# Handing over the spread of a norm's root one dense output behind the root, in a hybrid decoder block on Trainium2

## The chip, the core and the metric

The kernel runs on one core of one Trainium2 chip. A core has five engines that work side by side, each through its own instructions in order: TensorE (matmul; "PE" in the profile, "PEld" for its weight loads), VectorE ("DVE"), ScalarE ("ACT"), GpSimd ("POOL") and SyncE ("SP", which issues most DMAs). The metric is the device time of one execution in microseconds, less is better. Before the change it is 1903.87 us, the median of three runs (1902.76 to 1906.84).

## What is computed

One layer of a decoder on a sequence of 2048 tokens with 1024 features, all in float32. The reference, cut to the layer itself:

```python
hn = rmsnorm(h, norm1_g)
proj = jnp.einsum('bsd,de->bse', hn, w_in)          # u_pool | q | k | v, 512 each
y_pool = pool_mixer(u_pool, pool_w, pool_scale)     # causal means over 2, 4, 8, 16 tokens
o = stick_breaking_attention(to_heads(q), to_heads(k), to_heads(v))   # 8 heads of 64
mixed = jnp.concatenate([rmsnorm(y_pool, pool_out_g), rmsnorm(y_attn, attn_out_g)], axis=-1)
h = h + jnp.einsum('bse,ed->bsd', mixed, w_out)
hn2 = rmsnorm(h, norm2_g)
act = jnp.square(jax.nn.relu(jnp.einsum('bsd,df->bsf', hn2, w_up)))
h = h + jnp.einsum('bsf,fd->bsd', act, w_down)
return rmsnorm(h, final_g)
```

with `rmsnorm(x, g) = x * rsqrt(mean(x * x) + 1e-6) * g` over the features of a token.

## The kernel before

**Tiling.** The tokens are cut into four blocks j = 0 to 3 of 512. A tile holds 128 features by 512 tokens, so a block is eight such chunks. A float32 operand is split into a high part and a rest (`split`, lines 145 and 146: a ScalarE copy and a VectorE difference), and a product takes three matmuls of the parts (lines 177 to 179). A *dense output* is one chunk of an output: 8 x 3 matmuls into one PSUM buffer of the pool `psd`, which has two, and an evacuation of it. One step of the program makes one dense output.

**Phases.** `front(0)` projects blocks 0 and 1 (30 steps), `front(1)` blocks 2 and 3 (32 steps). The attention over near tokens (`near`), in units of two query blocks, is woven in between the dense outputs. `tail` multiplies by w_out, block after block (4 x 8 steps, evacuation on line 813). Then come the up and down products of the feed-forward part, some 1200 us, which the change does not touch.

**A norm.** The squares of the chunks are added up (`add_square`, lines 184 to 188). `mean_squares` sums over the features with eight small matmuls (`pm`, line 204). `inv_root` takes the inverse root: line 212 on VectorE fetches m from PSUM, and lines 213 to 223 are 13 small steps on GpSimd. Lines 240 and 241 split the root into `yr`. The *spread* (`spread`, line 230) is eight matmuls that copy each token's root to all 128 partitions (`pr`, in PSUM), and line 250 copies that on ScalarE to `r`. All this is `inv_rms`. The pieces that use r follow: `normed` (line 262: product with gain and root on VectorE, then a split and, for pool and attention norms, a write to `mx` on SP's queue) or the products of `norm2` (line 828). Thirteen norms have their root on GpSimd through `inv_rms`: norm1 of blocks 1, 2, 3, the pool norms and the attention norms of all four blocks, and norm2 of blocks 0 and 1. The first norm is on VectorE; norm2 of blocks 2 and 3 goes through `root_last`, and the final norms have code of their own.

**What sets the order.** Work that is not urgent goes as closures into the list `later`. After each step, `catch_up` takes some of them from its front: `state["pieces"]` (1, 2 or 3 by phase), but at least 2 while the list holds more than 8. At the ends of phases a note flushes the list whole. What a closure traces is put behind two earlier instructions on their engines (`issue_after`): the latest weight split and the evacuation of the output before the last. After `catch_up`, `advance` traces attention units, to be issued behind the last matmul of the step. The program is not run in the order of tracing: a planner that simulates the core's engines gives each engine its order beforehand. It prefers what was traced earlier, except that what is traced under `tc.high_priority()` comes as if from the program's start. All of `inv_rms` is traced so. `state["tick"]` counts up by 2 with a step. `gates` are bounds on the other side: no matmul of a dense output beyond that tick may be issued ahead of the named one (`pm` 10 ticks behind its root, `pr` 14). The PSUM buffers of `pr` come from `pst` (tag `pt`, two buffers, shared with the attention's transposes `pta`), or from `psz` with `early`.

Further names in the prediction: `pls` is the split pooled input of `pool_group` (matmuls on lines 396 to 398), `vf` and `ptv` a v chunk and its transposes (`keep_v`, lines 437 and 440), `sums_first` (lines 850 to 857) makes sums of normed chunks and writes them to `su`, which the up product reads as `sr`.

Of the kernel before, what the change touches and what calls it, by code (L numbers as in the profile page):

```python
# [17 lines left out]
D = 1024  # L18
# [27 lines left out]
def hymba_block(ctx: ExitStack, tc: tile.TileContext, xT, gains, w_in, pool_w, w_out, w_up, w_down, out):  # L46
    nc = tc.nc
# [103 lines left out]
    later = []  # L151
    marks, gates = {}, []
# [37 lines left out]
    def sum_tile():  # L190
        return tmp.tile([P, T], F32, tag="ss", name="ss", bufs=2)
# [7 lines left out]
    def mean_squares(parts, n, where=None, tag="px"):  # L199

        pm = (where or psx).tile([P, T], F32, tag=tag, name="pm")
        for c in range(TB):
            for i, ss in enumerate(parts):
                marks["pm"] = nc.tensor.matmul(pm[:, c:c + 1], ss[:, c * P:(c + 1) * P], inv[n],
                                               start=(i == 0), stop=(i == len(parts) - 1))
        return pm[:, 0:TB]

    def inv_root(pm, eng):

        v, w = vp.tile([P, 3 * TB], F32, tag="v", name="v"), pm.shape[-1]  # L210
        m, y, t = v[:, 0:w], v[:, TB:TB + w], v[:, 2 * TB:2 * TB + w]
        nc.vector.tensor_scalar(m, pm, 1.0, EPS, op0=ALU.mult, op1=ALU.add)
        eng.tensor_scalar(y.bitcast(I32), m.bitcast(I32), -0.5, float(0x5F3759DF), op0=ALU.mult, op1=ALU.add)
        for _ in range(3):
            if eng is nc.vector:
                eng.scalar_tensor_tensor(t, y, -0.5, y, op0=ALU.mult, op1=ALU.mult)
                eng.tensor_tensor(t, t, m, ALU.mult)
                eng.scalar_tensor_tensor(y, t, 1.5, y, op0=ALU.add, op1=ALU.mult)
            else:
                eng.tensor_tensor(t, y, y, ALU.mult)  # L220
                eng.tensor_tensor(t, t, m, ALU.mult)
                eng.tensor_scalar(t, t, -0.5, 1.5, op0=ALU.mult, op1=ALU.add)
                eng.tensor_tensor(y, y, t, ALU.mult)
        return y
# [9 lines left out]
    def inv_rms(ss, n, r=None, eng=None, early=False):  # L234

        eng = eng or nc.gpsimd
        with tc.high_priority():
            y = inv_root(mean_squares([ss], n, psz if early else None, "pz" if early else "px"), eng)
            yr = tmp.tile([P, 2, TB], F32R, tag="yr", name="yr")
            eng.tensor_copy(yr[:, 0], y)  # L240
            eng.tensor_tensor(yr[:, 1], y, yr[:, 0].bitcast(F32), ALU.subtract)
            where, tag = (psx, "px") if eng is nc.vector else (psz, "pz") if early else (pst, "pt")
            pr = where.tile([P, T], F32, tag=tag, name="pr")
            marks["pr"] = spread(pr, yr)
            if eng is not nc.vector:
                g = state["tick"]
                gates.extend([(g + 10, marks["pm"]), (g + 14, marks["pr"])])
            if r is None:
                r = tmp.tile([P, T], F32, tag="r", name="r", bufs=2)
            nc.scalar.activation(r, pr, AF.Copy)  # L250
            return r

    def rms(chunks):
        return inv_rms(sum_squares(chunks), len(chunks) * P)
# [41 lines left out]
    todo, begun, finished, state = [], {}, set(), {"gran": 0, "tick": 0, "due": 0.0}  # L296


    st = [{} for _ in range(NT)]
# [31 lines left out]
    def root_tile():  # L331
        return pa.tile([P, T], F32, tag="r1", name="r1")
# [15 lines left out]
    def norm1_rms(j):  # L348
        def square(k):
            if k == 0:  # L350
                st[j]["ss"] = sum_tile()
            add_square(st[j]["ss"], st[j]["x"][:, k], k == 0)
        later.extend(lambda k=k: square(k) for k in range(KD))
        later.append(lambda: st[j].update(r=inv_rms(st[j]["ss"], D, root_tile() if j == 2 else None, early=j == 1)))

    def norm1(j):
        st[j]["h"] = normed(KD, lambda k: st[j]["x"][:, k], g1, lambda: make_h(j), lambda: st[j]["r"])
# [48 lines left out]
    def norm_parts(j, part, g, at, make=None):  # L406

        def square(k):
            if k == 0:
                st[j]["sm"] = sum_tile()  # L410
            add_square(st[j]["sm"], part(k), k == 0)
        later.extend(lambda k=k: square(k) for k in range(4))
        where = lambda: olp.tile([P, T], F32, tag="ra", name="ra", bufs=1) if make else None
        later.append(lambda: st[j].update(rm=inv_rms(st[j]["sm"], D // 2, where())))
        if make:
            return lambda: normed(4, part, g, make, lambda: st[j]["rm"])
        normed(4, part, g, make_st, lambda: st[j]["rm"], mx[j][at:at + 4])
# [400 lines left out]
    def root_last(i, ss, where=None, tag="px"):  # L818
        y = inv_root(mean_squares([ss], D, where, tag), nc.gpsimd)
        nc.gpsimd.tensor_copy(yrlast[:, i, 0], y)  # L820
        nc.gpsimd.tensor_tensor(yrlast[:, i, 1], y, yrlast[:, i, 0].bitcast(F32), ALU.subtract)

    def norm2(j):
        acc = [st[j]["acc"][:, k] for k in range(KD)]
        later.append(lambda: root_last(0, st[j]["sh"]) if j == 2 else st[j].update(rh=inv_rms(st[j]["sh"], D)))

        def put(k):
            nc.vector.scalar_tensor_tensor(acc[k], acc[k], g2[:, k:k + 1], st[j]["rh"], op0=ALU.mult, op1=ALU.mult)
        if j in PAIRS[0]:
            later.extend(lambda k=k: put(k) for k in range(KD))  # L830
# [654 lines left out]
        if not todo:  # L1485
            state["due"] = 0.0

    def catch_up(n):
        for _ in range(n):
            with ExitStack() as behind:  # L1490
                for ins in (last_split[0], done[0]):
                    if ins:
                        behind.enter_context(tc.issue_after(ins.ins))
                later.pop(0)()

    def run():
        for n, emit, again in prog:
            if n:
                if again:
                    w = grans[state["gran"] - n:state["gran"]]  # L1500
                else:
                    w = weights(state["gran"], n)
                    state["gran"] += n
                state["tick"] += n
                with ExitStack() as behind:
                    for gate in [g for g in gates if g[0] < state["tick"]]:
                        behind.enter_context(tc.issue_after(gate[1].ins))
                        gates.remove(gate)
                    emit(w)
                catch_up(min(len(later), max(state["pieces"], 2 if len(later) > 8 else 1)))  # L1510
                advance(n / 2 * state["ratio"])
            else:
                emit()
        prog.clear()
# [61 lines left out]
    front(1)  # L1576
    tail(True)
    run()
    ffn()


    count = P * H * (TB * NT - 2)
    got = nc.values_load(zeros[0:1, 0:1], min_val=0, max_val=count)
# [59 lines left out]
```

## Time and profile before

| | us |
|---|---|
| time, median of three runs | 1903.87 |
| time of the profiled execution | 1905.2 |
| its span, first to last instruction | 1903.5 |
| granted TensorE clock over the span | 0.994 |
| the GpSimd roots' spreads, first and last start | 68.83 and 617.22 |

The page gives busy time and share by engine. A row of the timeline gives start, length, engine, line and operation, output and inputs, how many instructions it merges, and in brackets the idle time of the engine before it with what ended that. A row of the list of waits gives who waited for whom, the sum in us, the number of times and the longest. A row of the windows gives, for a stretch of the span, its length, each engine's busy time with its instructions (PE, PEld, DVE, ACT, POOL), the granted clock of TensorE (1.00 is full), the mean share of busy DMA engines and GB/s. Matmuls overlap, so a matmul's own length is longer than the distance to the next.

### The profile page before, as it was taken

The page shows a single profiled execution, that of the slowest core. Times are in us where ns is not written, and L with a number is a line of the kernel's source. Part 1 is how long each engine was busy: PE and PEld are TensorE (multiplying, and loading weights), DVE is VectorE, ACT ScalarE, POOL GpSimd, SP SyncE. Part 2 cuts the span into 40 slices and gives each one's busy share as a digit, 9 for nine tenths or more (in the row PEclk, how much of TensorE's full clock was granted, in tenths as well). Part 3 has the DMA queues.
Part 4 walks back from the last instruction along what each step waited for, and adds up shares of the span by engine and source line. Part 5 has one row for each costly group of instructions (what it writes and reads, how often), then busy time and mean ns, then how long its engine had stood idle before and what let it go on. Part 6 is the DMA issues. An engine that isn't in the chain of part 4 may idle for free.

```text
span 1903.5 us, 26682 instructions
## 1 busy us (share of the span) xinstructions
PE 1869.5 (98%) x8883; PEld 1555.5 (82%) x8883; DVE 1480.9 (78%) x2151; ACT 1023.7 (54%) x1616; POOL 242.1 (13%) x463
## 2 busy tenths in 40 slices
PE   9999999999999999999999999999999999999997
PEld 7888788888888888778888888887788888888886
DVE  6887799668866976778699988786566677888774
ACT  5565466555544465554557555554332665656543
POOL 0333233223421050000000000000010010020120
PEclk9999999999999999999999999999999999999998
DMA  6686696798788867887899888889999899999752
GB/s 224 204 269 196 191 308 213 239 322 278 272 316 306 296 229 254 284 306 276 286 365 334 313 300 278 301 284 326 378 311 326 289 322 301 334 297 342 290 210 91
DMA packets 222164, 535.91 MB, mean 282 GB/s; under 512 B 26048, under 2 KB 32192, under 8 KB 218176
## 3 DMA queue, kind: packets, MB, share of 16 engines
q1 hardware_dynamic: 217264, 525.46, 79.2%
q0 software_dynamic: 4608, 8.39, 2.4%
q8 instruction: 72, 1.18, 0.3%
q14 instruction: 76, 0.62, 0.1%
q10 hardware_dynamic: 144, 0.26, 0.0%
HBM read 349.46 MB, written 184.55 MB: 281 GB/s over the span
## 4 chain that ended last, share of the span: by engine, by line
PE 45%; DMA 6%; DVE 4%; issue 2%; ACT 1%; POOL 0%; SPq 0%; DVEq 0%; ACTq 0%
PE pb L1274 14%; PE pb L1451 12%; PE pY L1101 10%; PE pZ L1101 5%; PE pX L1101 2%; DMA ar<-sd 1%; DVE hw L146 1%; DMA ar<-sdi 1%; PE pb L1391 1%; DMA t<-in_w_down_dram 1%; DMA su<-hs 0%; DMA sd<-a 0%; DMA td<-t 0%; DMA sdi<-a 0%; DMA b<-in_w_down_dram 0%
## 5 line engine op out<-in xcount | busy, mean ns | idle before, releaser
L1101 PE MATMUL pY<-sa,hw 128*128 128x512 f32 x1536 | 366.3, 389 | 3.0 <-ACT u L1024 2.6
L1101 PEld LDWEIGHTS pY<-sa,hw 128*128 128x128 f32 x1536 | 288.0, 188 | 64.3 <-ACT u L1024 3.9
L1274 PE MATMUL pb<-ad,wd 128*128 128x512 f32 x1344 | 305.1, 389 | 0.3 <-DVE ad L146 0.3
L177 PE MATMUL pd<-h,hl 128*128 128x512 f32 x752 | 299.0, 398 | 3.5 <-DVE acc L813 2.0
L179 PE MATMUL pd<-h,hl 128*128 128x512 f32 x752 | 297.6, 396 | 0.0
L178 PE MATMUL pd<-h,hl 128*128 128x512 f32 x752 | 297.5, 396 | 0.0
L1274 PEld LDWEIGHTS pb<-ad,wd 128*128 128x128 f32 x1344 | 252.2, 188 | 53.1 <-DVE ad L146 0.7
L1451 PE MATMUL pb<-ad,wd 128*128 128x512 f32 x1104 | 253.9, 390 | 2.4 <-ACT ad L145 2.0
L1451 PEld LDWEIGHTS pb<-ad,wd 128*128 128x128 f32 x1104 | 206.5, 188 | 46.1 <-ACT ad L145 2.4
L146 DVE TENSOR_TENSOR ad<-ar,ad 128x1024 fp32r<-128x1024 f32 x160 | 193.9, 1220 | 44.6 <-ACT ad L145 44.2
L145 ACT ACTIVATE ad<-ar 128x1024 fp32r<-128x1024 f32 x160 | 168.2, 1053 | 95.2 <-PE pb L1451 32.0
L1101 PE MATMUL pZ<-sa,hw 128*128 128x512 f32 x768 | 187.0, 390 | 1.1 <-DVE a L1044 1.0
L1101 PEld LDWEIGHTS pZ<-sa,hw 128*128 128x128 f32 x768 | 143.7, 188 | 32.4 <-DVE a L1044 2.6
L177 PEld LDWEIGHTS pd<-h,hl 128*128 128x128 f32 x752 | 142.6, 190 | 31.8 <-issue 2.8
L145 ACT ACTIVATE hl<-raw 128x512 fp32r<-128x512 f32 x168 | 104.2, 631 | 116.2 <-PE pd L179 66.1
L179 PEld LDWEIGHTS pd<-h,hl 128*128 128x128 f32 x752 | 142.5, 189 | 28.2
L178 PEld LDWEIGHTS pd<-h,hl 128*128 128x128 f32 x752 | 142.5, 190 | 26.8
L146 DVE TENSOR_TENSOR hl<-raw,hl 128x512 fp32r<-128x512 f32 x168 | 113.9, 684 | 45.8 <-ACT hl L145 45.5
L1018 ACT ACTIVATE a<-a 128x512 f32<-128x512 f32 x96 | 60.1, 629 | 97.4 <-DVE a L1060 43.0
L146 DVE TENSOR_TENSOR hw<-rt,hw 128x512 fp32r<-128x512 f32 x128 | 86.3, 683 | 26.0 <-ACT hw L145 26.0
L145 ACT ACTIVATE wd<-wq 128x1024 fp32r<-128x1024 f32 x56 | 59.3, 1060 | 76.8 <-PE pb L1274 68.1
L146 DVE TENSOR_TENSOR wd<-wq,wd 128x1024 fp32r<-128x1024 f32 x56 | 68.4, 1221 | 34.2 <-ACT wd L145 34.2
(218 smaller groups left out, 2736.2 us busy)
## 6 DMA issues: line engine op xcount, KB each, us to landing
ar<-sd SPq DMA_DIRECT2D x96, 512.0 KB, 5.7
ar<-sdi SPq DMA_DIRECT2D x64, 512.0 KB, 5.8
rb<-in_w_up_dram SPq DMA_DIRECT2D x30, 1024.0 KB, 6.6
sd<-a SPq DMA_DIRECT2D x104, 256.0 KB, 5.1
raw<-in_w_in_dram SPq DMA_DIRECT2D x50, 512.0 KB, 4.8
sdi<-hr SPq DMA_DIRECT2D x96, 256.0 KB, 5.5
wr<-in_w_down_dram SPq DMA_DIRECT2D x48, 512.0 KB, 5.6
sd<-s SPq DMA_DIRECT2D x88, 256.0 KB, 4.7
```

The costliest lines, as they stand in the source:

```text
L145: nc.scalar.activation(hi, src, AF.Copy)
L146: return nc.vector.tensor_tensor(lo, src, hi.bitcast(F32), ALU.subtract)
L177: nc.tensor.matmul(ps, hl[:, 0, c], hi, start=(k == 0), stop=False)
L178: nc.tensor.matmul(ps, hl[:, 0, c], lo, start=False, stop=False)
L179: mm = nc.tensor.matmul(ps, hl[:, 1, c], hi, start=False, stop=(k == n - 1))
L1018: nc.scalar.activation(t, src, AF.Relu)
L1101: nc.tensor.matmul(t, w[:, wx, c], a[:, ax, c % 2], start=first and c == 0 and x == 0, stop=last and c == G - 1 and x == 2, skip_group_che ...
L1274: nc.tensor.matmul(b, t[:, wx, 2 * (kk % 2) + c, i * P:(i + 1) * P], a[:, ax, c], start=p in ("P1", "P5", "P2") and kk == 0 and c == 0 and ...
L1391: nc.tensor.matmul(b[:, cols], block(t, wx, c, n), a[:, ax, c, cols], start=False, stop=(i == 1 and c == 1 and x == 2), skip_group_check=True)
L1451: nc.tensor.matmul(ps[q, n], block(t, wx, c, n), left_[q][:, ax, c], start=(n_ in ("P1", "P3") and kk == 0 and c == 0 and x == 0), stop=(n ...
```

## The change

`inv_rms` is cut in two. For a root on GpSimd it now ends with `yr`; the spread, its gate and the copy to `r` stand in a new function `to_all`. A new function `later_rms` puts three entries into `later`: the root, an empty entry, and the spread. `catch_up` stops at an empty entry when it is called behind a step, and passes over it when a flush calls it. The gate of the spread is 12 ticks behind its own handing over, where it was 14 behind the root's. The norms on GpSimd that were handed over through `later` use `later_rms` instead.

```diff
             eng.tensor_tensor(yr[:, 1], y, yr[:, 0].bitcast(F32), ALU.subtract)
-            where, tag = (psx, "px") if eng is nc.vector else (psz, "pz") if early else (pst, "pt")
+            if eng is nc.vector:
+                return to_all(yr, r, psx, "px")
+            gates.append((state["tick"] + 10, marks["pm"]))
+            return yr
+
+    def to_all(yr, r, where, tag):
+        with tc.high_priority():
             pr = where.tile([P, T], F32, tag=tag, name="pr")
             marks["pr"] = spread(pr, yr)
-            if eng is not nc.vector:
-                g = state["tick"]
-                gates.extend([(g + 10, marks["pm"]), (g + 14, marks["pr"])])
+            if tag != "px":
+                gates.append((state["tick"] + 12, marks["pr"]))
             if r is None:
                 r = tmp.tile([P, T], F32, tag="r", name="r", bufs=2)
             nc.scalar.activation(r, pr, AF.Copy)
             return r
+
+    def later_rms(at, key, ss, n, r=lambda: None, early=False):
+
+        got = {}
+        where = (psz, "pz") if early else (pst, "pt")
+        later.append(lambda: got.update(yr=inv_rms(ss(), n, early=early)))
+        later.append(None)
+        later.append(lambda: at.update({key: to_all(got["yr"], r(), *where)}))
...
-        later.append(lambda: st[j].update(r=inv_rms(st[j]["ss"], D, root_tile() if j == 2 else None, early=j == 1)))
+        later_rms(st[j], "r", lambda: st[j]["ss"], D, lambda: root_tile() if j == 2 else None, j == 1)
...
-        later.append(lambda: st[j].update(rm=inv_rms(st[j]["sm"], D // 2, where())))
+        later_rms(st[j], "rm", lambda: st[j]["sm"], D // 2, where)
...
-        later.append(lambda: root_last(0, st[j]["sh"]) if j == 2 else st[j].update(rh=inv_rms(st[j]["sh"], D)))
+        if j == 2:
+            later.append(lambda: root_last(0, st[j]["sh"]))
+        else:
+            later_rms(st[j], "rh", lambda: st[j]["sh"], D)
...
-    def catch_up(n):
+    def catch_up(n, stop=False):
         for _ in range(n):
+            if later[0] is None:
+                later.pop(0)
+                if stop:
+                    return
+                continue
...
-                catch_up(min(len(later), max(state["pieces"], 2 if len(later) > 8 else 1)))
+                catch_up(min(len(later), max(state["pieces"], 2 if len(later) > 8 else 1)), True)
```

## The prediction

> **What bounds the kernel now.** I read the page first, then TensorE's list of waits from 62 to 690 us (the stretch in which all thirteen GpSimd roots of line 240 lie), then the timeline around each spread, then a table of windows for the clock.
>
> ```profile
> span 1903.5 us, 26682 instructions
> PE 1869.5 (98%) x8883; PEld 1555.5 (82%) x8883; DVE 1480.9 (78%) x2151; ACT 1023.7 (54%) x1616; POOL 242.1 (13%) x463
> ```
>
> TensorE is busy in 1869.5 of 1903.5 us, so an edit that only changes the order can win two things: idle time of TensorE, 34 us in all, and time in which TensorE works at a lower clock. The second does not show in a busy share. The list of waits (us in total, times, longest) says where the idle time of the front and the output phase lies:
>
> ```profile
> PE pp L396 <- ACT pls L145: 2.9, 3, 2.1
> PE pd L177 <- DVE acc L813: 2.0, 2, 1.8
> PE pr L230 <- POOL yr L240: 1.7, 1, 1.7
> PE pp L397 <- DVE pls L146: 1.4, 2, 1.2
> PE ptv L440 <- ACT vf L437: 1.3, 1, 1.3
> ...
> PE pr L230 <- POOL yr L241: 0.3, 1, 0.3
> ```
>
> TensorE waited for a root (yr, lines 240 and 241) at one place only, for 1.7 + 0.3 = 2.0 us. Here is that place, the norm of the attention output of block 1, on TensorE, VectorE and GpSimd:
>
> ```profile
> 445.69 0.95 PE L204 MATMUL pm<-inv,ss 128*128 128x1 f32 x8
> ...
> 456.20 0.33 PE L230 MATMUL pr<-identr,yr 128*128 128x128 f32 x1 [1.68 <-POOL yr L240]
> 456.82 1.76 PE L230 MATMUL pr<-identr,yr 128*128 128x128 f32 x7 [0.29 <-POOL yr L241]
> ```
> ```profile
> 447.56 1.29 DVE L146 TENSOR_TENSOR hl<-raw,hl 128x512 fp32r<-128x512 f32 x2 [1.18 <-ACT hl L145]
> 448.78 0.15 DVE L212 TENSOR_SCALAR v<-pm 128x4 f32<-128x4 f32 x1
> ```
> ```profile
> 449.02 0.19 POOL L213 TENSOR_SCALAR v<-v 128x4 int32<-128x4 int32 x1 [5.77 <-DVE v L212]
> ...
> 455.61 0.54 POOL L240 CAST yr<-v 128x4 fp32r<-128x4 f32 x1
> 456.23 0.53 POOL L241 TENSOR_TENSOR yr<-v,yr 128x4 fp32r<-128x4 f32 x1
> ```
>
> The mean was done at 446.6. VectorE took it over only at 448.8, behind two weight splits that themselves had waited 1.18 us. GpSimd then needed 7.7 us, from 449.02 to 456.76. TensorE's order of work was fixed beforehand, and it reached the spread at 456.20 - 1.68 = 454.5, 7.9 us behind the mean, so it stood there.
>
> What follows the wait is dearer than the wait. The table of windows gives length, busy time of each engine, granted clock (PEclk), DMA share and GB/s:
>
> ```profile
> 204.20:207.70 3.50, 0.77 (x4) 0.25 (x2) 3.50 (x6) 3.48 (x8) 1.82 (x3) 0.99 0.87 287
> 207.70:214.50 6.80, 6.23 (x15) 4.87 (x16) 5.60 (x11) 2.04 (x4) 1.02 (x1) 0.50 0.87 227
> 214.50:453.40 238.90, 235.77 (x1335) 201.23 (x1334) 188.44 (x277) 141.90 (x260) 69.61 (x143) 1.00 0.83 269
> 453.40:456.80 3.40, 1.44 (x10) 0.82 (x7) 2.32 (x4) 1.74 (x3) 3.09 (x9) 1.00 0.95 283
> 456.80:463.70 6.90, 6.88 (x24) 6.11 (x25) 4.04 (x7) 2.42 (x5) 0.55 (x1) 0.51 0.84 246
> ...
> 579.70:583.10 3.40, 1.61 (x8) 1.06 (x7) 3.40 (x6) 1.15 (x2) 0.00 (x0) 1.00 1.05 413
> ```
>
> Behind the wait TensorE runs 6.9 us at a clock of 0.51 and so loses 6.9 x 0.49 = 3.4 us. The same happened once before, at 207.7, behind the waits for pls (2.1 + 1.2 us), which has nothing to do with a root. A wait of 1.8 us at 581 (1.61 us busy of 3.40) did not lower the clock. So here the drop comes somewhere between 1.61 and 1.44 us busy in 3.4 us.
>
> The Trainium skill, "TensorE: Matmul & The Clock Gate", section "Why this matters for your kernels", says that gaps up to about 3 us between matmuls are safe, since the clock falls only after a whole idle window. The trace disagrees: 2.0 us of idle time in a 3.4 us window was followed by a clock of 0.51. By the page's rule the removed wait would be worth 2.0 us and no more; that is the second rival below.
>
> **The change part by part.** No instruction is added or removed. The helper is cut in two: mean, root and yr stay where they were, and the spread (8 matmuls with their 8 weight loads) with its ScalarE copy goes to the planner one dense output later; the empty entry between them ends that output's share of the deferred work. Everything behind it in the list moves too: the scaled pieces of the norm (a VectorE product, a ScalarE copy, a VectorE difference, and for pool and attention norms a write to mx on SP's queue), then line 828's products, then the sums of line 850 with their seven su writes each.
>
> I walked the list for every norm. Four of the thirteen roots are flushed whole (norm1 of blocks 1 and 2, pool norm of block 3, attention norm of block 3), so both halves still come together and nothing moves. Nine move. For the attention norm of block 1 the two extra entries keep the list above eight for one output longer, so the squares are handed out sooner and the root one output (5.4 us) *earlier*, while the spread comes one output *later*. The gate constant falls from 14 to 12 ticks, but is counted from a tick at least two later, so it binds no sooner for the nine.
>
> *The wait at 456.* The missing slack is 2.0 us; an earlier root or a later spread is worth 5.4 us each. Either covers it. Bounds: 0 (the spread keeps its place, see the first rival) to 2.0 + 3.4 = 5.4 us. I take 5.4, since this norm moves at both ends. What is late next is the norm's pieces, which go to mx and are read back in the output phase, more than four dense outputs (22 us) on, so nothing.
>
> *The wait at 582.9.* In the output phase the second norm of block 0 does this:
>
> ```profile
> 569.36 0.69 DVE L813 TENSOR_TENSOR acc<-pd,acc 128x512 f32<-128x512 f32 x1 [0.24 <-PE pd L179]
> ...
> 576.16 5.39 DVE L828 SCALAR_TENSOR_TENSOR acc<-acc,gains,r 128x512 f32<-128x512 f32 x8
> ...
> 582.07 0.68 DVE L813 TENSOR_TENSOR acc<-pd,acc 128x512 f32<-128x512 f32 x1
> ```
> ```profile
> 582.90 0.47 PE L177 MATMUL pd<-h,hl 128*128 128x512 f32 x1 [1.79 <-DVE acc L813]
> ```
>
> All eight products of line 828 stand ahead of the next output's evacuation (line 813), and TensorE waits 1.8 us for a PSUM buffer. With the change, products 5 to 7 are handed out behind that output and not ahead of it: 3 of 8, or 2.0 of 5.4 us, come off the front of the evacuation. That covers 1.8 us. Bounds 0 to 1.8; I take 1.8.
>
> *What the later handing costs.* Nearest rows for its cover, in block 2's output phase:
>
> ```profile
> 645.26 0.67 DVE L813 TENSOR_TENSOR acc<-pd,acc 128x512 f32<-128x512 f32 x1
> ...
> 652.10 0.69 DVE L813 TENSOR_TENSOR acc<-pd,acc 128x512 f32<-128x512 f32 x1 [0.23 <-PE pd L179]
> ...
> 657.54 0.69 DVE L813 TENSOR_TENSOR acc<-pd,acc 128x512 f32<-128x512 f32 x1 [1.00 <-PE pd L179]
> ```
> ```profile
> 648.89 0.82 SPq L857 DMA_DIRECT2D su<-acc  x1
> ...
> 655.27 2.20 SPq L938 DMA_DIRECT2D sr<-su  x3
> ```
> ```profile
> 691.40 2.88 PE L1101 MATMUL pY<-sa,hw 128*128 128x512 f32 x12
> ```
>
> One output lasts 657.54 - 652.10 = 5.4 us. The output evacuated at 645.26 had ended two outputs before 652.1, at 641.2, so its buffer came free 4.7 us later, with 0.7 us to spare. The sums move behind one more evacuation, which helps the evacuation, and the last su write moves from 648.9 to about 654.3. SP reads su from 655.3 and TensorE first needs it at 691.4: covered by 36 us. If that cover were gone, TensorE would wait at 691. New small waits in the nine reordered stretches I bound from both sides. At worst there is one more like the 1.3 us for vf with a half-clock stretch, 1.3 + 3.4 = 4.7 us; at best that 1.3 us goes too, -1.3. I take 1.0, nearest to a single such wait without a loss of clock.
>
> *Sum.* Against the profiled execution (1905.2 us, the span of 1903.5 and 1.7 around it): -2.0 - 3.4 - 1.8 + 1.0 = -6.2, so **1899.0 us**. The median shown is 1903.87, 1.3 lower, and the runs spread from 1902.76 to 1906.84. Some of them may not have had every half-clock stretch, so the gain against the median is put at 4.9 us, or 0.26%.
>
> **The rivals.**
>
> *It does nothing where it counts.* The spread is planned at high priority in both kernels, so the planner may put it where it thinks the root is ready, whenever it was handed over. Two other norms speak for this, with spreads 9.6 and 8.7 us behind their means, about as far as the root takes:
>
> ```profile
> 173.25 0.95 PE L204 MATMUL pm<-inv,ss 128*128 128x1 f32 x8
> ...
> 182.85 1.00 PE L230 MATMUL pr<-identr,yr 128*128 128x128 f32 x8
> ...
> 228.47 0.95 PE L204 MATMUL pm<-inv,ss 128*128 128x1 f32 x8
> ...
> 237.21 1.01 PE L230 MATMUL pr<-identr,yr 128*128 128x128 f32 x8
> ```
>
> Against it: the attention norm of block 1 has its root moved as well, and pieces and products keep ordinary places. Time: 1903.9. Chance 0.17.
>
> *The wait goes and the clock was not at stake.* If in ordinary executions the 2.0 us fall across two windows, there is no half-clock stretch to win. Time: 1905.2 - 2.0 - 1.8 + 1.0 = 1902.4. Chance 0.18. The page's rule above gives this same time.
>
> *Slower: the wait moves to ScalarE's queue.* The copy of line 250 waits for the spread, and ScalarE works in order. The profile has one such case:
>
> ```profile
> 356.03 0.60 ACT L250 ACTIVATE r<-pr 128x512 f32<-128x512 f32 x1 [3.38 <-PE pr L230]
> ...
> 358.98 0.58 ACT L437 ACTIVATE vf<-pd 128x512 f32<-128x512 f32 x1
> ```
> ```profile
> 359.62 0.55 PE L440 MATMUL ptv<-ident,vf 128*128 128x128 f32 x3 [1.30 <-ACT vf L437]
> ```
>
> ScalarE stood 3.4 us in front of the copy; the evacuation vf queued behind it, and TensorE then waited 1.3 us for vf. So it decides from about 3.4 - 1.3 = 2.1 us of standing. If the spreads move back on TensorE and the copies do not move on ScalarE, six norms of the attention stretch pay 1.3 us each, one of them with a half-clock stretch: 6 x 1.3 + 3.4 = 11.2. Time: 1905.2 - 7.2 + 11.2 = 1909.2. Against it: the copy is planned from the same spread. Chance 0.15.
>
> *More is won.* The half-clock stretch at 207.7 (waits 3.3 us, clock 6.8 x 0.50 = 3.4 us) also goes, because the order around it shifts. Handing order there is unchanged, which speaks against it. Time: 1899.0 - 6.7 = 1892.3. Chance 0.10.
>
> **How the numbers follow.** The forecast has chance 0.40 and a range of its own from 1896.5 to 1901. Something like 0.2%, 3.8 us, is what a measurement of this kernel can tell from no change, so "faster" ends at 1900.1 and "slower" begins at 1907.7. Faster: 0.34 of the forecast, 0.10 of the last rival, 0.02 of the second, 0.46. Same: 0.06 of the forecast, 0.16 of each of the first two, 0.01 of the third, 0.39. Slower: 0.15, the third and the worst bound of the new waits. The range from 1893 to 1907 leaves out half of the last rival and most of the third, under 0.2.
>
> **What would show it.** Right: no wait of pr for yr near 456 and no clock of 0.5 from 456.8 to 463.7; pm of that norm some 5 us sooner; products of line 828 split around an evacuation and no wait near 582.9; the stretch at 207.7 still there. Wrong: the spreads as far behind their means as now with a wait left, longer idle time of ScalarE ahead of line 250, or a stretch at half clock at a new place.

## The result, and the profile after

The changed kernel takes 1907.05 us (median of 20 runs, 1901.71 to 1913.88). The kernel before, run beside it, takes 1903.41 us (20 runs, 1898.31 to 1910.54). The ratio is 1.0019, 95% interval [1.0011, 1.0028]: 3.6 us slower, where 4.9 us faster was forecast. The profiled execution took 1906.65 us.

The head of the page of the changed kernel:

```profile
span 1904.9 us, 26673 instructions
...
PE 1870.1 (98%) x8883; PEld 1554.6 (82%) x8883; DVE 1480.8 (78%) x2151; ACT 1024.4 (54%) x1616; POOL 249.8 (13%) x463
```

The same work, with TensorE at the same share. GpSimd is busy 7.7 us longer with the same 463 instructions; the last section comes back to that. TensorE's list of waits from 62 to 690 us:

```profile
PE pta L676 <- DVE sg L671: 2.6, 1, 2.6
PE pp L409 <- ACT pls L145: 2.1, 1, 2.1
PE po L688 <- DVE at L146: 1.8, 1, 1.8
...
PE pp L410 <- DVE pls L146: 1.2, 1, 1.2
PE pta L676 <- ACT sq L187: 1.2, 1, 1.2
PE pz L629 <- DMA kw<-ks: 1.1, 1, 1.1
PE pz L629 <- issue: 1.0, 1, 1.0
PE pr L230 <- POOL yr L240: 0.5, 2, 0.3
```

Read against the list of before: the 1.7 us for yr, the 1.8 for the evacuation (then line 813, now 826) and the 1.3 for vf are gone. New are 2.6 and 1.8 us on the attention's matmuls (`pta`, the transposes of the weights; `po`, the product with v), and three waits of 1.0 to 1.2. The two large new ones stand 3.6 us apart. Here they are on TensorE in the changed kernel:

```profile
332.26 0.40 PE L179 MATMUL pd<-h,hl 128*128 128x512 f32 x1
332.49 0.28 PE L629 MATMUL pz<-kw,qa 128*128 128x256 f32 x1
...
337.14 0.51 PE L688 MATMUL po<-at,vw 128*64 128x128 f32 x4 [1.75 <-DVE at L146]
337.50 0.62 PE L676 MATMUL pta<-ident,sg 128*128 128x128 f32 x4
340.75 1.09 PE L676 MATMUL pta<-ident,sg 128*128 128x128 f32 x4 [2.64 <-DVE sg L671]
...
344.82 0.73 PE L177 MATMUL pd<-h,hl 128*128 128x512 f32 x1
```

A dense output ends at 332.5, and the next begins at 344.82: 12.3 us with 45 matmuls of the attention and the pooling between. Counted from 0, these are dense outputs 41 and 42. The same place before the change:

```profile
332.95 0.39 PE L179 MATMUL pd<-h,hl 128*128 128x512 f32 x1
333.17 0.28 PE L616 MATMUL pz<-kw,qa 128*128 128x256 f32 x1
...
337.79 0.50 PE L397 MATMUL pp<-pls,pw 128*128 128x512 f32 x1 [0.23 <-DVE pls L146]
...
338.39 0.50 PE L177 MATMUL pd<-h,hl 128*128 128x512 f32 x1
```

There it is 5.2 us (333.17 to 338.39) with 31 matmuls. Dense output 42 also needs a PSUM buffer of `psd`, which VectorE empties with the difference `qk`. VectorE, first after the change, then before it:

```profile
336.42 0.67 DVE L146 TENSOR_TENSOR at<-pta,at 128x512 fp32r<-128x512 f32 x1
337.02 0.67 DVE L146 TENSOR_TENSOR hl<-raw,hl 128x512 fp32r<-128x512 f32 x1
337.62 0.67 DVE L402 SCALAR_TENSOR_TENSOR pl<-s,u 128x512 f32<-128x512 f32 x1
338.22 1.21 DVE L662 TENSOR_TENSOR_SCAN pc<-sh,later_keys 128x512 f32<-128x512 f32 x1
339.36 0.65 DVE L146 TENSOR_TENSOR at<-pta,at 128x512 fp32r<-128x512 f32 x1
339.94 0.67 DVE L671 TENSOR_TENSOR sg<-sg,pc 128x510 f32<-128x510 f32 x1
340.53 1.21 DVE L662 TENSOR_TENSOR_SCAN pc<-sh,later_keys 128x512 f32<-128x512 f32 x1
...
343.82 0.69 DVE L146 TENSOR_TENSOR qk<-pd,qk 128x512 fp32r<-128x512 f32 x1
```
```profile
337.05 0.69 DVE L146 TENSOR_TENSOR pls<-pl,pls 128x512 fp32r<-128x512 f32 x1
337.66 0.68 DVE L146 TENSOR_TENSOR qk<-pd,qk 128x512 fp32r<-128x512 f32 x1
...
341.50 2.49 DVE L649 TENSOR_TENSOR_SCAN pc<-sh,later_keys 128x512 f32<-128x512 f32 x2
```

Before, `qk` ran ahead of the two scans, and dense output 42, from 338.39, covered them. After, the two scans and the differences `sg` that depend on them stand ahead of `qk`, and on TensorE the transposes and products that need them stand ahead of dense output 42, with nothing dense beside them. What TensorE waited for there is `at` (1.75 us) and `sg` (2.64 us); `qk` was done at 344.51 and cost it no wait of its own. VectorE has no gap in this stretch, as the windows of the changed kernel show (columns as in the prediction):

```profile
323.50:344.80 21.30, 16.66 (x99) 14.07 (x98) 21.21 (x31) 12.74 (x24) 11.36 (x10) 0.88 0.60 199
336.30:339.70 3.40, 0.97 (x8) 0.73 (x8) 3.40 (x6) 2.81 (x6) 3.40 (x3) 1.00 0.85 223
339.70:346.50 6.80, 5.50 (x19) 4.54 (x20) 6.71 (x11) 2.63 (x5) 2.51 (x4) 0.50 0.53 148
```

VectorE is busy 21.21 of 21.30 us. TensorE is busy 0.97 us of the 3.40 from 336.3 and then runs 6.8 us at half clock, as it did in the prediction's stretch at 456.8. That stretch itself is at full clock now:

```profile
456.80:463.70 6.90, 6.90 (x42) 5.96 (x41) 4.49 (x7) 4.52 (x8) 3.33 (x14) 1.00 0.93 261
```

To compare many runs I add up, over a stretch, by how much each matmul starts later behind the one before it than is usual behind a matmul of that one's shape (the median in the kernel before: 0.227 us behind a 128x512, for instance); an earlier start counts against it. This counts idle time and half clock alike; below it is "TensorE's lost time". In us:

| stretch | before | after |
|---|---|---|
| up to dense output 34 | 13.8 | 13.9 |
| dense outputs 35 to 51 | 4.2 | 9.7 |
| 52 to 61 (the root at 456) | 5.5 | 2.6 |
| 62 to 93 (output phase) | 2.8 | 1.3 |
| feed-forward part | 10.8 | 10.6 |

Both predicted gains are there, 2.9 us where 5.4 was forecast and 1.5 where 1.8 was. A loss of 5.5 us, for which the prediction had +1.0, stands ahead of them; 4.9 of it lie between the end of dense output 40 and the start of 42 (2.1 us before, 7.1 after).

### The profile page after: what moved, and what is told of

The parts are those of the page before. It is cut to its first block, busy times and chain, and to the rows that moved or that the text cites. A ratio compares the mean times of both kernels' runs of the same rounds, so it can differ in the third digit from the quotient of the medians.

```text
span 1904.9 us, 26673 instructions
## 1 busy us (share of the span) xinstructions
PE 1870.1 (98%) x8883; PEld 1554.6 (82%) x8883; DVE 1480.8 (78%) x2151; ACT 1024.4 (54%) x1616; POOL 249.8 (13%) x463
## 4 chain that ended last, share of the span: by engine, by line
PE 49%; DMA 5%; DVE 3%; issue 1%; ACT 1%; POOL 0%; SPq 0%; DVEq 0%; ACTq 0%
PE pb L1290 13%; PE pY L1117 13%; PE pb L1467 12%; PE pZ L1117 6%; PE pX L1117 3%; DMA ar<-sd 2%; DMA ar<-sdi 1%; PE pb L1407 1%; DMA su<-hs 0%; DVE hw L146 0%; DMA td<-t 0%; DMA sdi<-a 0%; DMA b<-in_w_down_dram 0%; DMA t<-in_w_down_dram 0%; DMA wr<-in_w_down_dram 0%
## 5 line engine op out<-in xcount | busy, mean ns | idle before, releaser
L1265 POOL DMA_DIRECT2D p<-hs x8 | 7.2, 950 | 681.6 <-DMA wr<-td 678.9
```

What stands on the lines that cost most here:

```text
L1265: nc.gpsimd.dma_start(t, hs[j][4 * half + n], accum_op=ALU.add)
```

## Experiments

All variants are the changed kernel with one addition, so that each norm can be given either form:

```diff
+SPLIT = {...}
...
-    def later_rms(at, key, ss, n, r=lambda: None, early=False):
+    def later_rms(at, key, ss, n, r=lambda: None, early=False, who=None):
+        if who not in SPLIT:
+            later.append(lambda: at.update({key: inv_rms(ss(), n, r(), early=early, whole=True)}))
+            return
```

`whole=True` is the body of `inv_rms` before the change. The names are `x` for norm1, `p` for the pool norm, `a` for the attention norm, `h` for norm2, each with its block. With SPLIT empty the order of every engine is that of before, with all thirteen norms that of the changed kernel (the expectation of e13 miscounts them as eleven). All runs are five rounds beside the kernel before.

**First: which norms lose?** Theory A: the loss comes from the waits in the reordered attention of `front(1)`, so only norms handed over there lose. Theory B: every later spread costs a little. Theory C: the loss is spread over the kernel by chance.

```diff
+SPLIT = {("x", 1), ("x", 2), ("p", 0), ("p", 1)}
```

> Only the norms handed over in front(0) (norm1 of blocks 1 and 2, pool norms of blocks 0 and 1) use later_rms; all others as before. Theory A (the loss comes from TensorE waits in the reordered attention stretch of front(1)): little here, the wait of 1.0 us for pz near 90.6 us that the changed kernel shows, so 0 to +1.5 us. Theory B (each later spread costs something wherever it stands, by ScalarE's copy and the pieces behind it): its share of +3.6 us by the number of norms moved, about +0.8 us. Theory C (the +3.6 us are an accident of the half-clock windows, the order costs nothing): 0.

Measured: 1903.06 against 1903.16 us, 0.9996 [0.9982, 1.001]. Four split norms, no loss.

```diff
+SPLIT = {("x", 3), ("p", 2), ("a", 0)}
```

> Only norm1 of block 3, the pool norm of block 2 and the attention norm of block 0 use later_rms. Theory A: here lies the loss; +6 to +9 us against before, with TensorE waits for sg, at, kw or sq between dense outputs 40 and 56 and a half-clock stretch there (in the changed kernel dense output 55 ends 9.7 us later than before). Theory B: about +1.2 us. Theory C: 0.

Measured: 1908.46, 1.0019 [1.0003, 1.0034]: the whole loss, though by this ratio (3.6 us) less than the 6 to 9 us that theory A expected.

```diff
+SPLIT = {("a", 1)}
```

> Only the attention norm of block 1 uses later_rms, the one whose spread TensorE waited for at 456 us. Theory A: the wait of 2.0 us goes, and with it the half-clock stretch (3.4 us) in the executions that had one: -2 to -5.4 us, no new wait of over 0.5 us. Theory B: no gain beyond the wait, -2 + 0.4, about -1.6 us. Theory C: 0 to -2 us.

Measured: 1900.68, 0.9984 [0.9969, 1.0]. TensorE's lost time from 52 to 61 falls from 5.5 to 0.6 us: the wait at 456 and its half clock are gone, as predicted. How they went was not as predicted. TensorE, VectorE and GpSimd in this run:

```profile
444.03 1.00 PE L206 MATMUL pm<-inv,ss 128*128 128x1 f32 x8
...
453.32 0.31 PE L232 MATMUL pr<-identr,yr 128*128 128x128 f32 x1
```
```profile
445.07 0.16 DVE L214 TENSOR_SCALAR v<-pm 128x4 f32<-128x4 f32 x1
447.38 1.29 DVE L148 TENSOR_TENSOR hl<-raw,hl 128x512 fp32r<-128x512 f32 x2 [2.15 <-ACT hl L147]
```
```profile
445.32 0.19 POOL L215 TENSOR_SCALAR v<-v 128x4 int32<-128x4 int32 x1 [2.78 <-DVE v L214]
```

VectorE's fetch of the mean now stands ahead of the two weight splits, at 445.07 in place of 448.78, so GpSimd starts 3.7 us earlier (445.32 against 449.02). The mean came 1.7 us earlier (444.03 against 445.69), not 5.4, and the spread starts 9.3 us behind it, where it was 10.5. The fetch followed the end of the mean by 0.04 us, where it was 2.1 us in before; that alone covers the 2.0 us that were missing. Counted in dense outputs neither root nor spread moved: in before, in e3 and in the changed kernel the mean stands between the starts of dense outputs 56 and 57, and the spread between those of 57 and 58.

```diff
+SPLIT = {("p", 3), ("a", 2), ("a", 3), ("h", 0), ("h", 1)}
```

> Only the norms of the output phase (pool norm of block 3, attention norms of blocks 2 and 3, norm2 of blocks 0 and 1) use later_rms. Theory A: the wait of 1.8 us for the evacuation near 583 us goes and nothing comes for it: -1 to -2 us. Theory B: +0.8 - 1.8, about -1 us. Theory C: 0 to -2 us.

Measured: 1900.44, 0.9985 [0.997, 1.0]. The wait for the evacuation near 583 is gone. So A stands as to the place: of the four parts e2 alone shows a loss. C falls by e2. B, a small cost of each norm, would fit the intervals of all four runs; it falls by e5 below, where one norm alone costs 4.2 us.

**Second: which of the three, and which gains are real?**

```diff
+SPLIT = {("x", 3)}
```

> Only norm1 of block 3 uses later_rms (handed over behind dense outputs 34 and 35, its pieces one output later up to output 39). Theory A1: this one norm is the loss, since the first new waits (po for at, pta for sg, TensorE from 333 to 343 us, with a half-clock stretch) stand at dense output 41, ahead of the other two norms' places: +2 to +6 us, the same waits near 333 to 343 us in its profile. Theory A2: the two later norms (pool of block 2, attention of block 0) carry it: within 1 us of before.

Measured: 1907.47 against 1903.88, 1.0022 [1.0012, 1.0032]. Norm1 of block 3 by itself costs 4.2 us [2.3, 6.1], by the ratio. The same place on TensorE shows it again:

```profile
336.70 0.80 PE L703 MATMUL po<-at,vw 128*64 128x128 f32 x4 [1.75 <-DVE at L148]
...
340.30 1.08 PE L691 MATMUL pta<-ident,sg 128*128 128x128 f32 x4 [1.94 <-ACT at L147]
```

```diff
+SPLIT = {("p", 2)}
```

> Only the pool norm of block 2 uses later_rms (root behind dense output 42, spread behind 43). Theory A1: no new wait at 333 to 343 us, 0 to +1 us, less if the wait at 456 us falls away through the shifted list. Theory A2: +1.5 to +4 us, with new waits behind dense output 43.

Measured: 1901.43, 0.9988 [0.9978, 0.9998].

```diff
+SPLIT = {("a", 0)}
```

> Only the attention norm of block 0 uses later_rms (root behind dense output 47, spread behind 48). Theory A1: 0 to +1 us, with at most the waits of 1.1 us each that the changed kernel has at 396 and 434 us; less if the wait at 456 us falls away. Theory A2: +1.5 to +4 us.

Measured: 1900.98, 0.9982 [0.9974, 0.9991].

```diff
+SPLIT = {("a", 1), ("h", 0), ("h", 1)}
```

> The attention norm of block 1 and norm2 of blocks 0 and 1 use later_rms, all others as before: the two parts that gained alone (0.9984 and 0.9985). Theory A (parts act where they stand and add up): about 0.9970, -5.5 us, no wait for yr at 456 us and none for the evacuation near 583 us. Rival (the gains were chance, or are shared): 0.9985 to 1.0.

Measured: 1899.14, 0.9979 [0.9968, 0.999]. So the pool norm of block 2 and the attention norm of block 0 lose nothing. They even win, though neither is the norm of the wait at 456: TensorE's lost time from 52 to 61 falls to 0.2 and 0.3 us with them too. As in e3, VectorE's fetch follows the end of the mean within 0.3 us in e6 and e7, where it was 2.1 us in before. The same wait can go only once, so these three gains do not add. (The two parts of e8 win at different places and may add: 0.9984 and 0.9985 together are 0.9969, which lies in its interval.)

**Third: what about norm1 of block 3 costs?** Theory P: its pieces, handed over one output later, collide with the attention. Theory S: the later spread does. Theory O: neither; any edit upstream makes the planner lay the attention between dense outputs 41 and 42 in another order. The first kernel keeps root and spread together and moves only the pieces, the second moves the spread and takes the first two pieces along with it:

```diff
+            if who == ("x", 3):
+                later.extend([None, lambda: None])
```

> Norm1 of block 3 alone: its spread is handed over with its root as before, but an empty entry and an idle entry behind it move its pieces one output later, as the change does. Theory P (the later pieces of this norm load VectorE where it is the limit): about +4 us, as e5. Theory S (the later spread is the cause): 0. Theory O (any edit upstream makes the planner rearrange the attention work between dense outputs 41 and 42, where nothing dense covers it, and the cost is that of a transposes' wait for VectorE and GpSimd there): here the planner again puts eight transposes late in that stretch, so +2 to +4 us with waits of po and pta there.

Measured: 1911.78 against 1903.95, 1.0036 [1.0022, 1.005].

```diff
-        later.append(lambda: at.update({key: to_all(got["yr"], r(), *where)}))
+        def rest():
+            at[key] = to_all(got["yr"], r(), *where)
+            later.pop(0)()
+            later.pop(0)()
+        later.append(rest)
```

> Norm1 of block 3 alone: its spread is handed over one output later, but the next pieces are taken with it, so that the pieces are back in step from the second on. Theory P: 0. Theory S: about +4 us. Theory O: the stretch between dense outputs 41 and 42 is arranged anew here too (eight transposes behind ten AV products), so +1 to +4 us with waits there.

Measured: 1907.84, 1.002 [1.0004, 1.0036]. Both lose. Between the end of dense output 40 and the start of 42 TensorE loses 7.5 us in e9 and 5.1 in e10, in two further orders of the same matmuls, with half clock for 10.2 and 3.4 us there. In e9 TensorE waits for `at` and `sg` again (2.08 and 3.13 us), in e10 for the pooled split `pls` (0.60 and 2.26 us). This speaks for O: neither P nor S by itself gives both results.

**Fourth: the change without that norm.**

```diff
+SPLIT = {("x", 1), ("x", 2), ("p", 0), ("p", 1), ("p", 2), ("p", 3), ("a", 0), ("a", 1), ("a", 2), ("a", 3), ("h", 0), ("h", 1)}
```

> All norms as in the change but norm1 of block 3, which stays as before. If that norm alone is the loss: -4 to -7 us against before (0.9965 to 0.998), no wait near 333 to 347, 456 and 583 us. If the loss is spread over the change: 0.9995 to 1.0015.

Measured: 1899.91, 0.9973 [0.996, 0.9985]: faster than both kernels. The stretch between 40 and 42 loses 2.15 us, as before.

```diff
+SPLIT = {("p", 2), ("a", 0), ("a", 1), ("h", 0), ("h", 1)}
```

> Pool norm of block 2, attention norms of blocks 0 and 1, norm2 of blocks 0 and 1 as in the change, the rest as before. The wait at 456 us can go only once, so the parts do not add up (-2.3, -3.4, -3.0, -2.9 alone): the wait with its half-clock stretch (-2 to -5.4) plus the evacuation's wait (-1.8), 0.9963 to 0.998.

Measured: 1899.77, 0.9977 [0.9964, 0.9991], the same within the intervals. The other norms bring nothing to be seen.

Without the one norm the change stood 5.1 us ahead, by the ratio; with it 3.6 behind: 8.7 us, where that norm alone cost 4.2. Two runs ask whether it also takes away the others' gains.

```diff
+SPLIT = {every norm}
```

> All eleven norms split, the instructions in the order of the changed kernel, to be set directly beside the kernel before. If the losses add (norm1 of block 3 alone +4.1 us, the others together -5.1): about -1, ratio 0.9995. If norm1 of block 3 takes the other norms' gains away, so that its loss stands alone: +3 to +5, ratio 1.0015 to 1.003, as the result gave.

Measured: 1906.63 against 1903.53, 1.0011 [0.9997, 1.0024]. This is the order of the changed kernel once more, and the interval overlaps that of the result.

```diff
+SPLIT = {("x", 3), ("a", 1), ("h", 0), ("h", 1)}
```

> Norm1 of block 3, attn norm 1 and the two h norms split. The second pair alone measured 0.9979, norm1 of block 3 alone 1.0022. If what each wins or loses adds: 1.0001, about 1903.5. If norm1 of block 3 rearranges the work of dense outputs 42 to 56 too, so that attn norm 1 has nothing left to win there: 1.0015 to 1.0025, and TensorE loses 9 to 11 us beyond the usual spacing between dense outputs 35 and 51, where the pair alone lost 4.0.

Measured: 1904.64, 1.0008 [0.9995, 1.0021]. TensorE loses 10.3 us from 35 to 51, 0.2 from 52 to 61 and 0.7 in the output phase: the gains survive beside the loss. The cost of norm1 of block 3 is then 4.2 us alone, 5.5 beside these three (1.0008 - 0.9979 = 0.0029) and 7.2 to 8.7 beside all (from 1.0011 or 1.0019 to 0.9973). With intervals of 2 to 5 us on each of these ratios one cost of some 5 to 6 us would fit them all; that it grows is not shown. The traces speak against it. In the five kernels that split norm1 of block 3 at this rate (after, e2, e5, e13, e14), TensorE has the same matmuls in the same order from the end of dense output 40 to the start of 42, and loses 7.06 to 7.08 us there. In the nine that hand it over as before (before, e1, e3, e4, e6, e7, e8, e11, e12) the order is that of before, and the loss 2.1 to 2.4 us.

**Last: the split, or the order that comes with it?** Line 1532 hands the planner attention units at a rate from `RATIO_FRONT`; its fourth entry holds for the first part of `front(1)`. (The expectation of e15 calls it a share of products on GpSimd. That was a misreading: it is the rate.) With another rate the attention stands in another order there, with and without the split.

```diff
-RATIO_FRONT = (0.3, 0.4, 0.15, 0.4, 0.4, 0.3)
+RATIO_FRONT = (0.3, 0.4, 0.15, 0.35, 0.4, 0.3)
+SPLIT = {("x", 3)}
```

> Norm1 of block 3 split, and the share of the attention's products that go on GpSimd in the fourth entry of RATIO_FRONT 0.35 in place of 0.4 (a planner's number, so that it lays the attention's matmuls behind dense outputs 40 and 41 in another order). To be set beside the next kernel, which has the same number and no split. If the loss of norm1 of block 3 hangs on where the planner happens to lay those matmuls: the two differ by something else than the 4.1 us, of either sign, and TensorE's time lost between dense outputs 41 and 42 goes with the order, not with the split. If the later spread itself costs: this one is 3 to 5 us over the next.

Measured: 1899.3, 0.9978 [0.9961, 0.9994].

```diff
-RATIO_FRONT = (0.3, 0.4, 0.15, 0.4, 0.4, 0.3)
+RATIO_FRONT = (0.3, 0.4, 0.15, 0.35, 0.4, 0.3)
+SPLIT = {}
```

> The order of before with 0.35 in place of 0.4 in the fourth entry of RATIO_FRONT, no norm split. If the stretch hangs on the order alone, this is anywhere from 0.997 to 1.004 of before, as e5 and e9 moved it by such amounts with edits that add no work. If only the split costs: within 0.1% of before, and 3 to 5 us under the kernel with the split and 0.35.

Measured: 1899.34, 0.9979 [0.9964, 0.9994]. With the split 1899.30, without it 1899.34: the norm that cost 4.2 us costs nothing here that these runs show. Resampling the two sets of 12 times puts the difference between -3.2 and 2.4 us, so a cost of 4.2 us is outside. TensorE's lost time between 40 and 42 is 1.7 and 0.7 us.

```diff
-RATIO_FRONT = (0.3, 0.4, 0.15, 0.4, 0.4, 0.3)
+RATIO_FRONT = (0.3, 0.4, 0.15, 0.35, 0.4, 0.3)
+SPLIT = {every norm}
```

> All norms split as in the changed kernel, with 0.35 in place of 0.4 in the fourth entry of RATIO_FRONT, so that the attention's matmuls between dense outputs 41 and 42 stand as in the run of norm1 of block 3 with 0.35. If the whole change loses only through the order that norm1 of block 3 gives that stretch at 0.4: as fast as with 0.35 alone, 1898 to 1901, ratio 0.997 to 0.9985. If with all norms split there is a second loss of some 4 us, as the whole change against the sum of its parts suggests: 1902 to 1904, ratio 0.999 to 1.0.

Measured: 1896.99 against 1904.22, 0.9962 [0.9948, 0.9976], from six runs, the fastest of all. The change that loses 3.6 us at 0.4 stands 7.2 us ahead of before at 0.35. At 0.35 alone the gain was 4.0 us by its ratio, so 3 us of this may be the change's own; the intervals overlap, so that is not shown. On VectorE `qk` is ahead of the scans again:

```profile
332.55 0.69 DVE L148 TENSOR_TENSOR pls<-pl,pls 128x512 fp32r<-128x512 f32 x1
333.16 0.68 DVE L148 TENSOR_TENSOR qk<-pd,qk 128x512 fp32r<-128x512 f32 x1
...
336.15 1.21 DVE L677 TENSOR_TENSOR_SCAN pc<-sh,later_keys 128x512 f32<-128x512 f32 x1
```

```diff
-RATIO_FRONT = (0.3, 0.4, 0.15, 0.4, 0.4, 0.3)
+RATIO_FRONT = (0.3, 0.4, 0.15, 0.35, 0.4, 0.3)
+SPLIT = {every norm but ("x", 3)}
```

> All norms but norm1 of block 3 split, with 0.35. If leaving out norm1 of block 3 wins only by keeping the old order between dense outputs 41 and 42: the same as the kernel before this one within 0.1%. If the split of norm1 of block 3 costs by itself: 4 to 8 us less than that one. If the gain of the number 0.35 and the gain of the other norms add: 1895; if both win the same wait at 456: 1898 to 1900.

Measured: 1899.82, 0.9981 [0.9967, 0.9995]. Leaving out norm1 of block 3, which won 7 to 9 us at 0.4, wins nothing at 0.35. So the loss is not in the later spread or the later pieces as such. It is in the order that they happen to bring about at one place. That this order loses by way of VectorE's full queue is read from the waits in the traces; no run moved those instructions alone. It also stays open why the planner prefers the bad order at 0.4: its own estimate of that stretch was not read.

TensorE's lost time, in us, beside the times:

| run | ratio | 35 to 51 | 52 to 61 | output phase |
|---|---|---|---|---|
| before | 1 | 4.2 | 5.5 | 2.8 |
| after | 1.0019 | 9.7 | 2.6 | 1.3 |
| e3, attn norm 1 | 0.9984 | 4.0 | 0.6 | 2.6 |
| e5, norm1 of 3 | 1.0022 | 10.5 | 6.0 | 3.5 |
| e9, its pieces | 1.0036 | 11.9 | 7.0 | 2.3 |
| e10, its spread | 1.002 | 7.8 | 5.3 | 3.8 |
| e11, all but it | 0.9973 | 6.0 | 1.3 | 2.5 |
| e13, all | 1.0011 | 11.9 | 6.2 | 2.5 |
| e15, norm1 of 3, 0.35 | 0.9978 | 2.0 | 1.0 | 4.0 |
| e17, all, 0.35 | 0.9962 | 2.5 | 0.9 | 1.4 |

One order of instructions does not give the same losses in each execution: after and e13 have the same on every engine, and differ by 3.6 us from 52 to 61. A wait of TensorE for ScalarE's `sq` took 1.16 us in the one (to 434.48) and 1.95 us in the other (to 436.05), and only in e13 do 6.8 us of half clock follow, from 437.1.

## Why the prediction was wrong

**The bound.** Right: the change could win only idle time and clock of TensorE, and it moved only these.

**The wait at 456: -2.0 - 3.4.** Right that both can go: in the profile of e3 TensorE's lost time there falls by 4.9 us where 5.4 was forecast, and the time of that run by 3.0 us [0, 5.9] by its ratio. The 3.4 us came from a single profile and stand at the dear end of what the runs show. In seven traces TensorE waits some 2 us or more for this root: behind that wait, before, e5 and e9 show 6.8 us of half clock, e1, e4 and e10 3.4 us, and e16 none. The changed kernel won back 2.9 us in its profile, and in e13, with the same order, nothing (5.5 us before, 6.2 there).

The reason was wrong. I had the root one output earlier and the spread one later; neither moved by an output. What counted was VectorE's fetch, ahead of two weight splits or behind them: 0.04 us behind the mean's end in e3, 2.1 us in before. The prediction quotes just these two rows (447.56 and 448.78) and says the fetch came "behind two weight splits"; it then sought the cure elsewhere.

**The wait at 582.9: -1.8.** It is gone, but the products are not split around the evacuation, as I said they would be. The changed kernel on VectorE:

```profile
577.28 5.38 DVE L844 SCALAR_TENSOR_TENSOR acc<-acc,gains,r 128x512 f32<-128x512 f32 x8
582.58 0.68 DVE L826 TENSOR_TENSOR acc<-pd,acc 128x512 f32<-128x512 f32 x1
...
585.87 2.07 DVE L275 SCALAR_TENSOR_TENSOR nt<-ol,gains,ra 128x512 f32<-128x512 f32 x3
```

All eight still stand ahead of it. What moved are three pieces of an attention norm (`nt`, 2.07 us). They ran ahead of the products in before, and now run behind the evacuation. This is their row in the kernel before, where the products begin at 576.16:

```profile
573.57 2.08 DVE L262 SCALAR_TENSOR_TENSOR nt<-ol,gains,ra 128x512 f32<-128x512 f32 x3
```

In e4, e8 and e12 too they run behind the evacuation, and the wait is gone. The size fits by luck: 2.07 us happens to cover 1.8.

**"New small waits in the nine reordered stretches I bound from both sides", taken as +1.0, at worst 4.7.** This is the step that failed. Where +1.0 us stands in the sum, norm1 of block 3 alone cost 4.2 us [2.3, 6.1] by e5, and 7.2 to 8.7 us beside all the others; in the trace it is 4.9 us between dense outputs 40 and 42. I priced a new wait as one more like the 1.3 us for vf, with a half-clock stretch at the worst. What came is a rearrangement: 14 more matmuls before dense output 42, two scans ahead of `qk` on VectorE, two waits of 1.75 and 2.64 us, and 6.8 us at half clock. A bound from the nearest *wait* did not hold that. Even the worst bound gives 1905.2 - 7.2 + 4.7 = 1902.7 us, so it could not carry the chance for "slower" that the prediction counts to it. The view for it was in the trace: VectorE busy without a gap in a part of `front(1)`, so that what the order puts into its queue there delays what stands behind (14.34 of 14.44 us from 323.95 to 338.39):

```profile
323.95:338.39 14.44, 13.40 (x82) 10.72 (x80) 14.34 (x22) 8.40 (x15) 3.79 (x6) 1.00 0.30 81
```

**The four norms that move nothing.** Norm1 of blocks 1 and 2, two of the four, are in e1, with 0.9996: no cost, as said.

**"The spread comes one dense output later."** Mostly it did not. In eight of the thirteen norms mean and spread begin behind the start of the same dense output as before, norm1 of block 3 among them; its spread follows the mean 10.9 us behind in the changed kernel and 9.5 us in before. First before, then after:

```profile
272.04 0.95 PE L204 MATMUL pm<-inv,ss 128*128 128x1 f32 x8
...
281.52 0.22 PE L230 MATMUL pr<-identr,yr 128*128 128x128 f32 x1
```
```profile
272.18 0.95 PE L204 MATMUL pm<-inv,ss 128*128 128x1 f32 x8
...
283.07 1.00 PE L230 MATMUL pr<-identr,yr 128*128 128x128 f32 x8
```

So what the edit moved was for the most part not the spread, but the order of the work handed over with and behind it.

**The rivals.** "It does nothing where it counts": fell, the waits went; but its reason, that the planner puts a spread where the root is ready whenever it was handed over, held in those eight norms. "The clock was not at stake": fell for the profiled executions, in which the stretch at 456.8 went from half to full clock and the new waits lowered the clock at 339.7; e16 shows that it can come out so. "Slower: the wait moves to ScalarE's queue": the sign came true, the mechanism did not, since the wait for vf is gone and the two large new ones are VectorE's; of the small ones one, 1.2 us for `sq`, is ScalarE's. "More is won": the waits for pls stayed, 2.1 and 1.2 us as before. The chance of 0.15 for slower was too small, because only one mechanism was let into it. With nine norms moved under a planner that reorders all that lies behind, an order that is worse somewhere deserved a rival of its own.

## What to carry to other kernels

Where a planner or a scheduler fixes the order, an edit that moves a few instructions is two edits: its own, and the new order of everything behind it. The second one can be the larger, and has either sign; here it cost 4 to 9 us by the times, against some 5 to be won. Run such a change with a neighbouring value of an unrelated knob as well, and part by part, before it is judged: at another rate of handing out work the same change was the fastest kernel of all. And look for the stretches in which the second engine has no gap: there each instruction that the order puts first delays all that the first engine needs behind it.

## What the hardware showed

**Half clock follows from little idle time, and its length is not set by the wait.** TensorE busy 0.97 of 3.40 us (336.3 to 339.7) gave 6.8 us at a clock of 0.50. That is 2.4 us of idle time in all; the rule of the Trainium skill weighed in the prediction, by which gaps up to about 3 us are safe ("TensorE: Matmul & The Clock Gate", section "Why this matters for your kernels"), fails here again. In e5 less was enough:

```profile
333.20:336.60 3.40, 1.75 (x16) 1.45 (x14) 3.40 (x7) 3.40 (x7) 3.40 (x2) 1.00 0.25 29
```

Then came 10.2 us at 0.50. In before 1.61 us busy of 3.40 lowered nothing, so the bound that the prediction read off its one profile, a drop between 1.44 and 1.61 us busy, does not hold for the other runs. As to the length: for the root at 456 TensorE waited 2.0 us in before and 3.8 us in e4, and ran at half clock for 6.8 and 3.4 us. The waits for pls, 2.1 and 1.2 us in both kernels, gave 6.8 us before, but only 3.4 in the changed kernel:

```profile
209.99:213.43 3.44, 3.44 (x9) 2.48 (x9) 3.44 (x8) 1.73 (x3) 0.15 (x1) 0.51 0.86 237
213.43:216.80 3.37, 3.37 (x16) 2.77 (x15) 1.98 (x5) 0.64 (x1) 0.00 (x0) 1.00 0.73 185
```

In the twenty traces every half-clock stretch from the first matmul to the last is 3.4, 6.8 or 10.2 us long.

**GpSimd stands still beside some of VectorE's instructions.** In the changed kernel, same operation, same shape:

```profile
336.49 3.15 POOL L660 TENSOR_SCALAR_AFFINE_SELECT sg<-sg 128x256 f32<-128x256 f32 x1
...
341.68 0.40 POOL L660 TENSOR_SCALAR_AFFINE_SELECT sg<-sg 128x256 f32<-128x256 f32 x1
```

The select took 0.40 us or 3.15. The long one ended at 339.64, 0.28 us after VectorE came to `at<-pta` (339.36), behind `hl`, `pl` and a scan, which all have two inputs in SBUF; `at` has one in PSUM. The Trainium skill, "SBUF — State Buffer", section "Who interferes with whom", says that a VectorE instruction with two SBUF inputs contends with a GpSimd instruction that reads SBUF, and that one with at most one SBUF input, outside the modes that use two ports, does not. The trace agrees in the main: of the GpSimd instructions that begin beside a VectorE `TENSOR_TENSOR` with two inputs in SBUF, 98 of 109 take over 1.3 times the shortest of their operation and shape, and 11 of 77 beside one with an input in PSUM. The long select is not all explained: it began at 336.49 beside an `at` (336.42) and was not done with it. Over the kernel GpSimd's busy time grows from 242.1 to 249.8 us with no instruction added; the selects make up 4.6 us of that:

```profile
L660 POOL TENSOR_SCALAR_AFFINE_SELECT sg<-sg 128x256 f32<-128x256 f32 x64 | 61.6, 964 | 195.2 <-ACT sg L637 187.3 <-DMA kw<-ks 7.9
```

The 64 selects take 964 ns in the mean (892 ns, 57.0 us in all, in the kernel before), where the free one takes 0.40 us.
